# Layer 0's output product: seven half-size products for the prompt tiles, a plain one for the sample tile

## The chip, the core and the metric

The kernel runs on one core of one Trainium2 chip. A core has a matrix engine (TensorE, "PE" in the profile, with its weight loads as "PEld"), a vector engine (VectorE, "DVE"), a scalar engine (ScalarE, "ACT"), GpSimd ("POOL") and SyncE ("SP"), which issues the DMAs. Each works through its own queue in order; waits on semaphores tie the queues together. Operands lie in SBUF, 128 partitions wide; PE writes its results to PSUM, eight banks of 512 float columns, called `PB[0]` to `PB[7]`. The metric is the device time of one execution in microseconds (us).

## What is computed

One step of a two-layer encoder on 512 prompt rows and 128 sample rows (8 requests of 16). Layer 0 is a gated MLP, layer 1 an attention layer. After its mixer each layer multiplies by an output matrix, norms the result, adds it to the residual, and adds a gated embedding:

```python
def gmlp_branch(h, w_in, ln_g, ln_b, w_s, b_s, w_out):
    ...
    y = u * s.reshape(B, T, E) * jax.nn.silu(z)
    return y @ w_out, v
...
        xp = xp + rms_norm(op, norm_post[i])
        xs = xs + rms_norm(os_, norm_post[i])
        xp = xp + jax.nn.sigmoid(xp @ ple_w_gate[i]) * (p_prompt[i] @ ple_w_proj[i])
        xs = xs + jax.nn.sigmoid(xs @ ple_w_gate[i]) * (p_sample[i] @ ple_w_proj[i])
```

The change is about `y @ w_out` of layer 0: y has 640 rows (five tiles of 128: tiles 0 to 3 the prompt, tile 4 the sample) and 2048 columns, `w_out` is 2048 x 1024.

## The kernel before

All products are made from float32 values cut into a coarse part ("hi") and a rest ("lo"). `split` (L272 and L273) does it: ACT copies the source into a rounded type, DVE subtracts the copy from the source. `mm3` (L258 to L260) then issues three matmuls, hi by hi, hi by lo and lo by hi; each loads 128 columns of the left operand as weights of the array and streams up to 512 columns of the right one.

**Weights.** All weight blocks of the program stand in one list, `units`, in the order of use; a block is 256 rows by 512 columns (or 512 by 256) of float32, 512 KB. `fetch` issues its DMA (L119) into one of three raw buffers (`RAW`), `prefetch` splits it into one of five buffers in `W` (hi and lo, 1024 columns each), and `weights(n)` hands out the next n and asks for as many more as there are free buffers. So PE works on one buffer while up to four more are filled.

**Layer 0's mixer** is computed in pairs of 128-column groups, whose left factors are themselves made by seven half-size products: the sums of weight blocks are made by POOL (L200), the sums of results by DVE (L540 to L555). The last operations of a group are `gate_spatial` (L565 to L579), which leaves y in `R`, transposed: for each of 16 groups g of 128 columns of y a block of 128 partitions by 640 rows, `y0_at(g)`. The layout is that of the left operand, so a tile's 128 columns can be loaded as weights directly.

**The output product** is the first part of `tail(0, ...)`. For each half h of the 1024 output columns it runs over eight weight blocks (`kk`), in each over five row tiles t and two 128-row slices j of the block: 2 x 8 x 5 x 2 calls of `mm3`, accumulated in five PSUM banks. Before a block, `split_y` splits the y groups that it will need, each of 640 columns; each is split twice, once per half h. Ten transposes of the embedding input `p_prompt`, `p_sample` (L631) and five splits of it lie at the start of the product.

**Behind it** come, per tile: the squares and their sum (ACT, L704), the reciprocal root (DVE and POOL, L280 and L282), two scalings (DVE, L708, L709), two additions to the residual (L710, L711), eight transposes (L296) and their splits; then the product of the embedding (`embed`, 12 matmuls a tile), the gate product (48 matmuls a tile in two halves), and the norm in front of layer 1.

What decides the order on an engine is not the text alone: a scheduler places the instructions on each engine's queue along a modelled timeline, within what the data allow. `order` in the listings below is the result of that for one engine. Buffers come free in the order of use, so a late split holds up the DMA behind it, and a late matmul the split behind it.

Of the kernel before, what the change touches and what calls it, by code (L numbers as in the profile page):

```python
# [17 lines left out]
F32 = mybir.dt.float32  # L18
# [6 lines left out]
P = 128  # L25
D = 1024
# [31 lines left out]
def hybrid_trunk(tc, x_prompt, x_sample, ck, cv, clf, p_prompt, p_sample, norm_pre, norm_post,  # L58
# [19 lines left out]
    def second(name, dt):  # L78

        pool = tc.alloc_tile_pool(name=name, bufs=1, reuse_waits="tile")  # L80
        return pool, pool.tile([P, 10240], dt, name=name + "_t")
# [8 lines left out]
    def r1(o, n, p=P):  # L90
        return R1[:p, o:o + n]

    def f(ap):
        return ap.bitcast(F32)
# [3 lines left out]
    def ring(name, lst):  # L98
        i = counters.get(name, 0)
        counters[name] = i + 1  # L100
        return lst[i % len(lst)]

    def bank(lst=(0, 1, 2, 3, 4, 5, 6, 7)):
        return PB[ring(("bank", lst), lst)]

    def small(n=1, keep=False):

        name, first, end = ("kept", 0, 172) if keep else ("small", 172, N_SMALL)
        i = counters.get(name, first)
        if i + n > end:  # L110
            assert not keep
            i = first
        counters[name] = i + n
        return SML[:, i:i + n]
# [3 lines left out]
    def dma(out, in_):  # L118
        behind["sp"] = nc.sync.dma_start(out=out, in_=in_)  # L119
# [12 lines left out]
    def u_rows(w, r0, c0, k, n):  # L132
        units.append((w[r0:r0 + k * P, c0:c0 + n].rearrange("(k p) n -> p k n", p=P), k))
# [9 lines left out]
    def u_tail(wout, layer):  # L143
        for h in range(2):
            for kk in range(8):
                u_rows(wout[0], kk * 256, h * 512, 2, 512)
        for h in range(2):
            u_rows(w_proj[layer], 0, h * 512, 2, 512)
        for h in range(2):
            for kk in range(4):  # L150
                u_rows(w_gate[layer], kk * 256, h * 512, 2, 512)

    u_tail(g_wout, 0)
    joined = set()
    for p in range(8):
        for part in (2, 1, 0, 3):
# [8 lines left out]
    S0, S1 = 16, 48  # L165
    items = []
    for i in range(len(units)):
        if not S0 <= i < S1:
            items.append((i, None))
        elif i % 2 == 0:  # L170
            items += [(i, j) for j in range(4)]

    n0 = S1 + 16 + 2 + 8
    few = range(n0, n0 + 64 + 12)
    place, last_use = [], [-1] * (2 * NW)
    state = {"raw": 0, "used": 0}

    def raw_of(i):
        if S0 <= i < S1:
            z = (i - S0 + 1) % 4  # L180
            if z == NRAW:
                return r1(o_X, 1024)
        else:
            z = i % NRAW if i < S0 else (i + 1) % NRAW
        return RAW[:, z * 1024:z * 1024 + 1024]

    def fetch(upto):
        while state["raw"] < min(upto, len(units)):
            ap, k = units[state["raw"]]
            dma(raw_of(state["raw"]).rearrange("p (k n) -> p k n", k=k), ap)  # L190
            state["raw"] += 1

    def left_operands(i, j):
# [6 lines left out]
                nc.gpsimd.tensor_tensor(out=o, in0=a, in1=b, op=op)  # L200
        return (a11, SF[:, :1024], SF[:, 1024:2048], raw_of(i + 1))[j]

    def prefetch(upto, i0=0):

        while len(place) < min(upto, len(items)):
            i = len(place)
            u, j = items[i]
            taken = {z for k in range(i0, i) for z in place[k]}
            step = 1 if j == 0 else 2
            free = [z for z in range(0, 2 * (NW - (u in few)), step) if not taken & set(range(z, z + step))]  # L210
            if not free:
                return
            z = min(free, key=lambda z: max(last_use[z:z + step]))
            place.append(range(z, z + step))
            last_use[z:z + step] = [i] * step
            fetch(u + 1 if j is None else u + 2)
            o, n = z * 1024, step * 512
            hi, lo = W[:, o:o + n], W[:, o + n:o + 2 * n]
            if u in joined:
                k = units[u][1]  # L220
                hi, lo = (W[:, o:o + 2 * n].rearrange("p (k z n) -> p z k n", z=2, k=k)[:, z] for z in range(2))
                split(hi, lo, raw_of(u).rearrange("p (k n) -> p k n", k=k))
            elif j is None:
                split(hi, lo, raw_of(u))
            else:
                split(*((x.rearrange("p (k n) -> p k n", k=4) for x in (hi, lo)) if j == 0 else (hi, lo)), left_operands(u, j))
                if u > S0:
                    fetch(u + 4)

    def weights(n):  # L230

        i0 = state["used"]
        state["used"] += n
        prefetch(i0 + 2 * NW, i0)
        res = []
        for i in range(i0, i0 + n):
            u, j = items[i]
            k, o, m = units[u][1], place[i][0] * 1024, len(place[i]) * 512
            if u in joined:
                res.append(W[:, o:o + 2 * m].rearrange("p (k n) -> p k n", k=k))  # L240
                continue
            if j in (1, 2):
                views = [W[:, o + z:o + z + m].rearrange("p (a k n) -> p k a n", a=2, k=k) for z in (0, m)]
            else:
                views = [W[:, o + z:o + z + m].rearrange("p (k n) -> p k n", k=k) for z in (0, m)]
            res.append(tuple(views))
        return res
# [8 lines left out]
    def mm3(out, lhs, rhs, start, stop):  # L256
        (lh, ll), (rh, rl) = lhs, rhs
        nc.tensor.matmul(out, lh, rh, start=start, stop=False)  # L258
        nc.tensor.matmul(out, lh, rl, start=False, stop=False)  # L259
        nc.tensor.matmul(out, ll, rh, start=False, stop=stop)  # L260
# [9 lines left out]
    def split(hi, lo, src):  # L270

        nc.scalar.activation(out=hi, in_=src, func=AF.Copy)  # L272
        nc.vector.tensor_tensor(out=lo, in0=src, in1=f(hi), op=ALU.subtract)  # L273

    def rstd_of(ss, eps, mean=False, keep=False):
        t = small()
        if mean:
            nc.vector.tensor_scalar(out=t, in0=ss, scalar1=eps, scalar2=None, op0=ALU.add)
        else:
            nc.vector.tensor_scalar(out=t, in0=ss, scalar1=1.0 / D, scalar2=eps, op0=ALU.mult, op1=ALU.add)  # L280
        q = small(keep=keep)
        nc.gpsimd.tensor_tensor(out=q, in0=t, in1=mhalf, op=ALU.pow)  # L282
        return q

    def tok_rows(prompt, sample, t):
        return prompt[t * P:(t + 1) * P] if t < 4 else sample
# [42 lines left out]
    def run(steps):  # L329

        while True:
            try:
                next(steps)
            except StopIteration as e:
                return e.value
# [15 lines left out]
    def r2(o, n, p=P):  # L351
        return R2[:p, o:o + n]
# [173 lines left out]
    def y0_at(g):  # L526

        return r1(g // 4 * 2560, 2560).rearrange("p (t n) -> p t n", t=NT)[:, :, (g % 4) * P:(g % 4 + 1) * P]
# [207 lines left out]
                    xn = r1(o_xn + (t % 2) * D, D)  # L736
                    norm_to_hT(x1[t], xn, xn, gpre, t, (5, 6, 7))

    tail(0, lambda g, half: y0_at(g), (0, 1, 2, 3, 4))


    PRJ, ATT = (0, 1, 2, 3), (4, 5, 6)
# [428 lines left out]
```

## Time and profile before

| | us |
|---|---|
| median of 3 runs | 1315.37 (1315.31 to 1315.43) |
| the profiled execution: its own time | 1315.17 |
| the profiled execution: span from the first to the last instruction | 1313.4 |
| DVE busy in the span | 794.1 |
| ACT busy in the span | 553.1 |
| POOL busy in the span | 136.1 |

The mean granted clock of TensorE is 0.997 of the full one. The profile shows one execution: for each engine its busy time; windows of time with the busy time of each engine in them; groups of instructions of one line, operation and shape with their mean time; the timeline of single instructions; and the chain that ended last, which goes back from the end from each step to the one that released it. In a row `L273 DVE TENSOR_TENSOR W<-RAW,W 128x1024` stands for line 273, executed by DVE, writing the tile W from RAW and W, with 128 partitions and 1024 columns. `R` is the large buffer `R1`, `pb` a PSUM bank, `sf` and `r2x_t`, `r2b_t` are uses of a second buffer, `SML` holds scalars, one to a partition. A busy interval can overlap the next one of the same engine by a little.

### The profile page before, as it was taken

What the parts mean: (1) busy time and instruction counts of PE and PEld (TensorE: products, weight loads), DVE (VectorE), ACT (ScalarE), POOL (GpSimd) and SP (SyncE); (2) the same over time, 40 slices, a digit from 0 to 9 for tenths busy, and PEclk for the clock granted to TensorE, in tenths of its full rate; (3) what the DMA queues carried; (4) which work ended last, traced back from release to release, by engine and by line L of the source; (5) the groups of instructions that cost most, each with busy time, mean ns of one, the idle gap of its engine ahead of it and who ended that gap; (6) DMA issues with size and microseconds to landing.
All of it is one profiled execution on the core that took longest, in us unless ns stands there. A gap on an engine that the chain in (4) does not pass through costs nothing.

```text
span 1313.4 us, 20355 instructions
## 1 busy us (share of the span) xinstructions
PE 1304.7 (99%) x7683; PEld 1152.3 (88%) x7683; DVE 794.1 (60%) x1671; ACT 553.1 (42%) x1074; POOL 136.1 (10%) x144
## 2 busy tenths in 40 slices
PE   8999999999999999999999999999999999999998
PEld 6888999999988888888999889898988988888887
DVE  7744999999844455644555554556555566554543
ACT  5334555444535343533433334333434344435431
POOL 1012454543000000000000000000000000000100
PEclk8999999999999999999999999999999999999999
DMA  6432333232424213589676665788557687343211
GB/s 227 132 108 67 120 118 121 86 104 73 129 94 149 79 49 113 167 135 149 152 194 151 155 160 148 165 150 171 132 150 163 149 213 235 113 132 132 66 56 57
DMA packets 300053, 172.79 MB, mean 132 GB/s; under 512 B 188785, under 2 KB 269473, under 8 KB 299954
## 3 DMA queue, kind: packets, MB, share of 16 engines
q1 hardware_dynamic: 299810, 171.23, 49.3%
q8 instruction: 60, 0.98, 0.3%
q14 instruction: 39, 0.32, 0.1%
q10 hardware_dynamic: 144, 0.26, 0.1%
HBM read 149.86 MB, written 21.59 MB: 131 GB/s over the span
## 4 chain that ended last, share of the span: by engine, by line
PE 95%; DVE 3%; DMA 1%; issue 1%; ACT 0%; SPq 0%; POOL 0%; DVEq 0%
PE pb L258 22%; PE pb L260 22%; PE pb L259 22%; PE pb L324 7%; PE pb L867 6%; PE pb L325 3%; PE pb L868 3%; PE pb L986 3%; PE pb L979 1%; PE pb L1040 1%; PE pb L1066 1%; PE pb L296 1%; DVE W L273 1%; PE pb L571 1%; PE pb L1063 1%
## 5 line engine op out<-in xcount | busy, mean ns | idle before, releaser
L273 DVE TENSOR_TENSOR W<-RAW,W 128x1024 fp32r<-128x1024 f32 (+1 forms) x156 | 193.5, 1242 | 170.8 <-ACT W L272 136.5
L272 ACT ACTIVATE W<-RAW 128x1024 fp32r<-128x1024 f32 (+1 forms) x156 | 161.0, 1033 | 151.0 <-PE pb L260 47.5
L258 PE MATMUL pb<-A,W 128*128 128x384 f32 (+1 forms) x640 | 221.8, 347 | 0.0
L260 PE MATMUL pb<-A,W 128*128 128x384 f32 (+1 forms) x640 | 208.7, 326 | 0.0
L259 PE MATMUL pb<-A,W 128*128 128x384 f32 (+1 forms) x640 | 208.3, 325 | 0.0
L258 PE MATMUL pb<-W,A 128*128 128x512 f32 x520 | 205.0, 395 | 2.3 <-ACT A L272 2.3
L259 PE MATMUL pb<-W,A 128*128 128x512 f32 x520 | 203.7, 392 | 0.0
L260 PE MATMUL pb<-W,A 128*128 128x512 f32 x520 | 203.3, 393 | 0.1
L324 PE MATMUL pb<-A,W 128*128 128x512 f32 x384 | 150.7, 393 | 0.0
L258 PEld LDWEIGHTS pb<-A,W 128*128 128x128 f32 x640 | 120.4, 188 | 18.7 <-issue 8.9
L259 PEld LDWEIGHTS pb<-A,W 128*128 128x128 f32 x640 | 121.0, 189 | 0.7
L260 PEld LDWEIGHTS pb<-A,W 128*128 128x128 f32 x640 | 120.2, 188 | 0.1
L258 PEld LDWEIGHTS pb<-W,A 128*128 128x128 f32 x520 | 98.1, 189 | 22.3 <-ACT A L272 2.5
L867 PE MATMUL pb<-W,A 128*128 128x512 f32 x320 | 116.6, 403 | 0.0
L260 PEld LDWEIGHTS pb<-W,A 128*128 128x128 f32 x520 | 97.9, 188 | 20.9 <-DVE A L273 0.6
L259 PEld LDWEIGHTS pb<-W,A 128*128 128x128 f32 x520 | 98.0, 188 | 19.4
L325 PE MATMUL pb<-A,W 128*128 128x256 f32 x384 | 107.7, 280 | 0.0
L868 PE MATMUL pb<-W,A 128*128 128x256 f32 x320 | 89.5, 280 | 0.0
L273 DVE TENSOR_TENSOR A<-R,A 128x640 fp32r<-128x640 f32 (+1 forms) x51 | 41.0, 836 | 71.4 <-ACT A L272 70.7
L867 PEld LDWEIGHTS pb<-W,A 128*128 128x128 f32 x320 | 60.0, 188 | 15.1 <-DVE R L872 2.6
L325 PEld LDWEIGHTS pb<-A,W 128*128 128x128 f32 x384 | 72.1, 188 | 0.4 <-issue 0.4
L324 PEld LDWEIGHTS pb<-A,W 128*128 128x128 f32 x384 | 72.1, 188 | 0.2
(252 smaller groups left out, 2285.8 us busy)
## 6 DMA issues: line engine op xcount, KB each, us to landing
RAW<-in_fox_w_in SPq DMA_DIRECT2D x64, 512.0 KB
RAW<-in_gmlp_w_in SPq DMA_DIRECT2D x40, 512.0 KB
r2b_t<-in_cache_fox_v SPq DMA_DIRECT2D x32, 512.0 KB
r2b_t<-in_cache_fox_k SPq DMA_DIRECT2D x128, 128.0 KB
RAW<-in_gmlp_w_out SPq DMA_DIRECT2D x16, 512.0 KB
RAW<-in_ple_w_gate SPq DMA_DIRECT2D x16, 512.0 KB
RAW<-in_fox_w_out SPq DMA_DIRECT2D x16, 512.0 KB
out<-R SPq DMA_DIRECT2D x42, 128.0 KB
```

The costliest lines, as they stand in the source:

```text
L258: nc.tensor.matmul(out, lh, rh, start=start, stop=False)
L259: nc.tensor.matmul(out, lh, rl, start=False, stop=False)
L260: nc.tensor.matmul(out, ll, rh, start=False, stop=stop)
L272: nc.scalar.activation(out=hi, in_=src, func=AF.Copy)
L273: nc.vector.tensor_tensor(out=lo, in0=src, in1=f(hi), op=ALU.subtract)
L296: nc.tensor.transpose(out=b[:, j * P:(j + 1) * P], in_=src[:, (4 * c + j) * P:(4 * c + j + 1) * P], identity=ident)
L324: nc.tensor.matmul(out[1].rearrange("p (z n) -> p z n", z=2), w[0], h_both[:, :, k, SA:], start=k == 0, stop=False)
L325: nc.tensor.matmul(out[1][:, :TOK - SA], w[1], h_hi[:, k, SA:], start=False, stop=k == 7)
L571: nc.tensor.matmul(b0[:, t * P:(t + 1) * P], v_at(pnl, t)[:, c0:c0 + P], wm, start=True, stop=True)
L867: nc.tensor.matmul(b, hi, w, start=k == 0, stop=False)
L868: nc.tensor.matmul(b[:, :256], lo, w[:, :256], start=False, stop=k == 7)
L986: nc.tensor.matmul(O[:, d], v[:, j, hh * P:(hh + 1) * P], pt[:, j * P:(j + 1) * P], start=(j == 0), stop=(j == i))
```

## The change

The output product of layer 0 is made by a new function, `tail7`, in place of `tail(0, ...)`; layer 1 keeps `tail`. The four prompt tiles are taken as two halves (tiles 0 and 1, tiles 2 and 3), the 2048 columns of y as two halves, and the 1024 output columns as two halves. The product of these 2 x 2 by 2 x 2 blocks is made from seven half-size products instead of eight, with sums of blocks of y on the one side, sums of blocks of `w_out` on the other, and sums of results. A half-size product has 2 tiles x 8 slices, 16 calls of `mm3`. The sample tile is multiplied plainly, from the blocks that are there anyway.

The seven products come in three groups of 2, 3 and 2, each in four steps (`kk`). A step needs 3, 4 and 2 blocks of `w_out` (named by column half and row half, "21" is the second column half and the first row half), 36 blocks in all for 16 before. POOL makes the sums of weight blocks, in place, in the raw buffers (`out_operand`), which are eight now: three in `RAW` and five in a new use `r2o_t` of the second buffer; the first six blocks use `RAW` alone. DVE makes three of the four sums of y blocks (`sum1`, `sum3`, `sum2`), POOL the fourth (`sum4`, three operations). `parts_of` splits them into one of the slots in `A`. ACT and DVE bring results from PSUM to SBUF and add them up (`leave`). Tiles 2 and 3, complete after the second group, are normed during the last step but one of the third group.

```diff
+    def u_out7(wout):
+        for names in (("11", "21", "22"), ("11", "21", "22", "12"), ("12", "22")):
+            for kk in range(4):
+                out7[len(units)] = names
+                for n in names:
+                    u_rows(wout[0], ((int(n[1]) - 1) * 4 + kk) * 256, (int(n[0]) - 1) * 512, 2, 512)
...
     def raw_of(i):
-        if S0 <= i < S1:
+        if S2 <= i < S3:
+            z = (i - S2 + 1) % 3 if i < S2 + 6 else (i - S2 - 6 + 3) % 8
+            if z >= NRAW:
+                return r2((z - NRAW) * 1024, 1024)
+        elif S0 <= i < S1:
...
+    OUT_NEEDS = {"out30": 1, "out31": 3, "out40": 2, "out41": 3, "out42": 4, "out20": 1, "out21": 2}
+
+    def out_operand(u, j):
+        a = [raw_of(u + z) for z in range(len(out7[u]))]
+        sums = {"out31": (2, 1, 2, ALU.add), "out40": (1, 0, 1, ALU.subtract), "out41": (2, 2, 1, ALU.subtract),
+                "out42": (3, 3, 2, ALU.subtract)}
+        if j not in sums:
+            return a[int(j[-1])]
+        o, x, y, op = sums[j]
+        nc.gpsimd.tensor_tensor(out=a[o], in0=a[x], in1=a[y], op=op)
+        return a[o]
...
-            fetch(u + 1 if j is None else u + 2)
+            fetch(u + 1 if j is None else u + OUT_NEEDS.get(j, 2))
...
+            elif j in OUT_NEEDS:
+                split(hi, lo, out_operand(u, j))
...
-    tail(0, lambda g, half: y0_at(g), (0, 1, 2, 3, 4))
+    def tail7(layer, y_at):
...
+        def b_of(k, i, j):
+            return y_at(k + 8 * i)[:, 2 * j:2 * j + 2]
+        def sample_of(k, i):
+            return y_at(k + 8 * i)[:, 4:]
...
+        def sum1(k):
+            return parts_of(combine(nc.vector, scratch(), b_of(k, 0, 1), b_of(k, 0, 0)))
+        def sum3(k):
+            t3[k] = combine(nc.vector, scratch(), b_of(k, 1, 1), b_of(k, 0, 1))
+            return parts_of(t3[k])
+        def sum2(k):
+            return parts_of(combine(nc.vector, t3[k], t3[k], b_of(k, 0, 0), ALU.add))
+        def sum4(k):
+            o = combine(nc.gpsimd, scratch(), b_of(k, 1, 0), b_of(k, 1, 1))
+            combine(nc.gpsimd, o, o, b_of(k, 0, 1), ALU.add)
+            return parts_of(combine(nc.gpsimd, o, o, b_of(k, 0, 0)))
+        plain = lambda i, j: lambda k: parts_of(b_of(k, i, j))
+        stages = (
+            (((plain(0, 0), (0, 1)), (lambda k: parts_of(sample_of(k, 0)), (4,))), ((sum1, (2, 3)),)),
+            (((sum3, (0, 1)), (lambda k: parts_of(sample_of(k, 0), True), (4,))), ((sum2, (5, 6)),), ((plain(1, 1), (2, 3)),)),
+            (((lambda k: parts_of(sample_of(k, 1)), (7,)), (plain(1, 0), (5, 6))),
+             ((lambda k: parts_of(sample_of(k, 1)), (4,)), (sum4, (0, 1)))))
...
+        def leave(s, part):
+            for t in range(2):
+                if (s, part) == (0, 0):
+                    nc.scalar.activation(out=c_of(t, 0), in_=PB[t], func=AF.Copy)
+                elif (s, part) == (0, 1):
+                    nc.scalar.activation(out=c_of(t + 2, 1), in_=PB[2 + t], func=AF.Copy)
+                elif (s, part) == (1, 1):
+                    add(c_of(t + 2, 0), c_of(t, 0), PB[5 + t])
+                    add(c_of(t, 1), c_of(t + 2, 0), PB[t])
+                    add(c_of(t + 2, 0), c_of(t + 2, 0), c_of(t + 2, 1))
+                    add(c_of(t + 2, 1), c_of(t + 2, 1), c_of(t, 1))
+                elif (s, part) == (1, 2):
+                    add(c_of(t + 2, 0), c_of(t + 2, 0), PB[2 + t])
...
+        def out_steps():
...
+                            for _, banks in part:
+                                while len(left) < min(n + 9, len(todo)):
+                                    fn, k = todo[len(left)]
+                                    left.append(fn(k))
...
+                                for t, o in enumerate(banks):
+                                    ts = slice(t * P, (t + 1) * P)
+                                    mm3(PB[o], (hi[:, ts], lo[:, ts]), (w[0][:, j], w[1][:, j]), first, done)
...
+                    if (s, kk) == (2, 2):
+                        for t in (2, 3):
+                            normed(t)
...
+    tail7(0, y0_at)
```

The lines of the changed program stand elsewhere: `split` is L314 and L315, `mm3` L300 to L302, the sums of weight blocks L240, the sums of y blocks L844, the negative split of the sample L825 and L826, the sums of results L872, the gating L607 to L621 (L565 to L579 before). Three places in the queues follow.

DVE just ahead of the product; `L574` and `L616` are the same operation, the first gating of the last pair of groups. Before:

```order
L273 TENSOR_TENSOR W_63<-RAW_66,W_63 128x1024
L540 TENSOR_TENSOR R1_69<-R1_69,pb2_72 128x320
L273 TENSOR_TENSOR A_65<-R1_69,A_65 128x640 x2
L589 SCALAR_TENSOR_TENSOR R1_69<-sf_223,R1_69 128x320
L540 TENSOR_TENSOR R1_69<-R1_69,pb3_73 128x320
L574 SCALAR_TENSOR_TENSOR R1_69<-pb4_74,SML_68,sf_223 128x4x128
```

The same place in the changed program:

```order
L315 TENSOR_TENSOR W_63<-RAW_66,W_63 128x1024
L582 TENSOR_TENSOR R1_69<-R1_69,pb1_71 128x320
L631 SCALAR_TENSOR_TENSOR R1_69<-sf_223,R1_69 128x320
L315 TENSOR_TENSOR A_65<-R1_69,A_65 128x128
L315 TENSOR_TENSOR A_65<-R1_69,A_65 128x256 x2
L315 TENSOR_TENSOR A_65<-R1_69,A_65 128x128
L582 TENSOR_TENSOR R1_69<-R1_69,pb2_72 128x320
L631 SCALAR_TENSOR_TENSOR R1_69<-sf_223,R1_69 128x320
L582 TENSOR_TENSOR R1_69<-R1_69,pb3_73 128x320
L616 SCALAR_TENSOR_TENSOR R1_69<-pb4_74,SML_68,sf_223 128x4x128
```

The splits of whole y groups have become splits of two tiles (256 columns) and of the sample tile (128 columns).

DVE in the product, `W` the weight buffers and `A` the slots for parts of y. Before, early in it, with the embedding's splits (`pb5`, `pb6`, `pb7`) still among them:

```order
L273 TENSOR_TENSOR W_63<-RAW_66,W_63 128x1024
L273 TENSOR_TENSOR A_65<-pb6_76,A_65 128x2x128
L273 TENSOR_TENSOR A_65<-pb7_77,A_65 128x2x128
L273 TENSOR_TENSOR A_65<-R1_69,A_65 128x640 x2
L273 TENSOR_TENSOR W_63<-RAW_66,W_63 128x1024
```

In the changed program, where the splits for the second group begin:

```order
L315 TENSOR_TENSOR W_63<-r2o_t_2985,W_63 128x1024
L826 SCALAR_TENSOR_TENSOR A_65<-R1_69,A_65 128x128
L315 TENSOR_TENSOR A_65<-r2o_t_2985,A_65 128x256
L826 SCALAR_TENSOR_TENSOR A_65<-R1_69,A_65 128x128
L315 TENSOR_TENSOR W_63<-r2o_t_2985,W_63 128x1024
L844 TENSOR_TENSOR r2o_t_2985<-r2o_t_2985,R1_69 128x256
L315 TENSOR_TENSOR A_65<-r2o_t_2985,A_65 128x256 x2
L315 TENSOR_TENSOR A_65<-R1_69,A_65 128x256
L844 TENSOR_TENSOR r2o_t_2985<-r2o_t_2985,R1_69 128x256
L315 TENSOR_TENSOR W_63<-r2o_t_2985,W_63 128x1024
```

Between two weight splits stand about as many operations as before, of smaller shape, and PE has 12 or 18 matmuls to a weight split where it had 30.

POOL from the last sum of the mixer's weights on. Before, it next makes the reciprocal roots behind the product:

```order
L200 TENSOR_TENSOR sf_223<-R1_69 128x512
L200 TENSOR_TENSOR sf_223<-R1_69,RAW_66 128x512
L200 TENSOR_TENSOR sf_223<-sf_223,R1_69 128x512
L200 TENSOR_TENSOR sf_223<-RAW_66,sf_223 128x512
L282 TENSOR_TENSOR SML_68<-SML_68 128x1 x9
```

In the changed program stand behind the same four sums six sums of weight blocks, and then:

```order
L240 TENSOR_TENSOR r2o_t_2985<-r2o_t_2985 128x1024 x3
L240 TENSOR_TENSOR RAW_66<-RAW_66 128x1024
L240 TENSOR_TENSOR RAW_66<-RAW_66,r2o_t_2985 128x1024
L240 TENSOR_TENSOR r2o_t_2985<-r2o_t_2985,RAW_66 128x1024
L240 TENSOR_TENSOR r2o_t_2985<-r2o_t_2985 128x1024 x2
L844 TENSOR_TENSOR r2o_t_2985<-R1_69 128x256 x2
L240 TENSOR_TENSOR r2o_t_2985<-r2o_t_2985 128x1024
L844 TENSOR_TENSOR r2o_t_2985<-r2o_t_2985,R1_69 128x256
```

All 40 of POOL's new sums stand there, 16 of weight blocks and 24 of y blocks, where it had none in the product.

More of the change, by code (lines that the diff above doesn't have):

```diff
@@ L151, in u_tail, with u_embed @@
                 u_rows(w_gate[layer], kk * 256, h * 512, 2, 512)
-    u_tail(g_wout, 0)
+    out7 = {}
+    def u_out7(wout):
[4 more added lines that the diff above has]
+                    u_rows(wout[0], ((int(n[1]) - 1) * 4 + kk) * 256, (int(n[0]) - 1) * 512, 2, 512)
+    def u_embed(layer):
+        for h in range(2):
+            u_rows(w_proj[layer], 0, h * 512, 2, 512)
+        for h in range(2):
+            for kk in range(4):
+                u_rows(w_gate[layer], kk * 256, h * 512, 2, 512)
+    S2 = len(units)
+    u_out7(g_wout)
+    S3 = len(units)
+    u_embed(0)
+    S4 = len(units)
     joined = set()
@@ L167, in hybrid_trunk @@
     for i in range(len(units)):
-        if not S0 <= i < S1:
+        if S2 <= i < S3:
+            if i in out7:
+                items += [(i, "out%d%d" % (len(out7[i]), z)) for z in range(3 if len(out7[i]) == 4 else 2)]
+        elif not S0 <= i < S1:
             items.append((i, None))
@@ L171, in hybrid_trunk @@
             items += [(i, j) for j in range(4)]
-    n0 = S1 + 16 + 2 + 8
-    few = range(n0, n0 + 64 + 12)
+    few = range(S4, S4 + 64 + 12)
     place, last_use = [], [-1] * (2 * NW)
@@ L178, in raw_of @@
     def raw_of(i):
-        if S0 <= i < S1:
+        if S2 <= i < S3:
+            z = (i - S2 + 1) % 3 if i < S2 + 6 else (i - S2 - 6 + 3) % 8
+            if z >= NRAW:
+                return r2((z - NRAW) * 1024, 1024)
+        elif S0 <= i < S1:
             z = (i - S0 + 1) % 4
```

123 lines of the change are left out of this document (added).

## The prediction

> **What bounds the kernel now.** I read the page first, for which engine is full, then the windows of the stretch that the change touches, and last the chain that ended last inside it.
>
> ```profile
> span 1313.4 us, 20355 instructions
> PE 1304.7 (99%) x7683; PEld 1152.3 (88%) x7683; DVE 794.1 (60%) x1671; ACT 553.1 (42%) x1074; POOL 136.1 (10%) x144
> 346.30:456.70 110.40, 110.40 (x495) 91.39 (x494) 51.01 (x68) 42.97 (x69) 1.48 (x2) 1.00 0.34 113
> ```
>
> The first two rows are the page's: TensorE (PE) is busy in 99% of the span. The third is a row of the windows (length, then PE, weight loads, DVE, ACT and POOL busy, granted clock, DMA share, GB/s): in the 110.4 us of layer 0's output product PE never rests, DVE works 51 us, ACT 43, POOL 1.5. So today this stretch lasts as long as its matmuls. A busy PE is no measure of its speed; the chain gives the step:
>
> ```profile
> 346.54 0.23 PE pb L258
> 346.77 0.23 PE pb L259
> ...
> 351.10 0.23 PE pb L260
> 351.33 0.45 PE pb L258 x2
> ```
>
> From 346.54 to 351.33 lie 21 matmuls of 512 columns: 0.228 us each. The product has 2 halves x 8 weight blocks x 5 tiles x 2 x 3 = 480 of them, 109.4 us; with the ten transposes of the embedding input (1.1 us) it starts at 346.54 and ends near 457.1.
>
> **What the change removes.** Five tiles by sixteen row blocks by two column halves were 160 triples. Now seven products of two tiles by eight blocks are 112 and the sample 32: 144 triples, 432 matmuls. 48 x 0.228 = **10.9 us less of PE**. If PE stayed the bound, that would be the whole answer, so the question is whether the other engines keep up with 98.5 us of matmuls.
>
> **What it adds.** Steps of DVE come from these rows; a reported DVE time overlaps the next one by 0.08 (1.21 at 244.87, next start 246.00), so a step is the mean less 0.08.
>
> ```profile
> L273 DVE TENSOR_TENSOR W<-RAW,W 128x1024 fp32r<-128x1024 f32 x25 | 30.6, 1225 | 19.4 <-ACT W L272 18.4
> L920 DVE SCALAR_TENSOR_TENSOR R<-R,r2b_t 128x256 f32<-128x256 f32 x16 | 6.8, 425 | 4.5 <-ACT R L919 3.9
> L579 DVE TENSOR_TENSOR R<-R 128x640 f32<-128x640 f32 x16 | 13.8, 861 | 0.0
> L710 DVE TENSOR_TENSOR R<-R 128x512 f32<-128x512 f32 x10 | 6.9, 687 | 0.0
> L708 DVE SCALAR_TENSOR_TENSOR R<-pb,SML,R 128x512 f32<-128x512 f32 x10 | 7.5, 749 | 0.9 <-POOL SML L282 0.8
> L1033 POOL TENSOR_TENSOR R<-R,CST 128x16 f32<-128x16 f32 x16 | 4.3, 267 | 164.6 <-DMA R<-cs_sc 164.6
> L272 ACT ACTIVATE W<-RAW 128x1024 fp32r<-128x1024 f32 x16 | 16.8, 1048 | 11.6 <-PE pb L260 11.1 <-ACT R L704 0.5
> ```
>
> Weight operands: 16 splits become 28, 1.14 us of DVE each. Tile operands: instead of 32 splits of 640 columns there are 56 of 256 columns (0.34, as L920) and 32 of 128 (0.20, see 251.16 below), and 24 sums of 256 (0.34). POOL, idle here so far, gets 16 sums of 1024 columns and 24 of 256. No POOL sum of these widths has been run; between 16 columns (0.267, L1033) and 512 (1.30, next fence) a column costs 2.08 ns, which gives 2.36 and 0.77 us. From below they cannot cost less than the 1.30 and 0.27 of those smaller rows; from above, two sums of 512 are 2.60, one of 512 is 1.30. I take the line between the two rows. By engine all this still fits into 98.5 us: DVE some 85, POOL 56, ACT 28 x 1.05 and the small copies, near 65. DMA rises from 16 to 36 blocks of 512 KB.
>
> **But DVE and POOL don't work side by side.** The next rows are the timeline of a stretch in which both run (start, duration, engine, line), DVE first and POOL below.
>
> ```profile
> 244.87 1.21 DVE L273 TENSOR_TENSOR W<-sf,W 128x1024 fp32r<-128x1024 f32 x1
> 246.00 0.47 DVE L540 TENSOR_TENSOR R<-R,pb 128x320 f32<-128x320 f32 x1
> ...
> 247.97 1.96 DVE L273 TENSOR_TENSOR W<-RAW,W 128x1024 fp32r<-128x1024 f32 x1 [0.50 <-ACT W L272]
> 249.85 0.87 DVE L540 TENSOR_TENSOR R<-R,pb 128x320 f32<-128x320 f32 x2
> 250.64 0.59 DVE L512 SCALAR_TENSOR_TENSOR sf<-sf,SML,R 128x128 f32<-128x128 f32 x1
> 251.16 0.28 DVE L513 TENSOR_TENSOR R<-CST,R 128x128 f32<-128x128 f32 x1
> 251.36 0.34 DVE L512 SCALAR_TENSOR_TENSOR R<-R,SML 128x128 f32<-128x128 f32 x1
> ...
> 247.55 1.30 POOL L200 TENSOR_TENSOR sf<-sf,RAW 128x512 f32<-128x512 f32 x1
> 248.92 2.16 POOL L200 TENSOR_TENSOR sf<-RAW,sf 128x512 f32<-128x512 f32 x1
> ```
>
> The weight split issued at 247.97, in the middle of a POOL sum, takes 1.96 instead of 1.22 and ends 1.08 after that sum (248.85): it stood still until POOL was through. The next sum is issued at 248.92, during the split, and takes 2.16 instead of 1.30: it ends 1.23 after the split's step (249.85). L512 then takes 0.59 instead of 0.34, waiting for POOL again. The two L540, which read a PSUM bank, run at their usual pace beside POOL. So a DVE operation with two SBUF inputs and a POOL sum exclude each other and take turns; their times add. [...]
>
> Nearly all that the change adds to DVE has two SBUF inputs. By block pair, in us, beside PE:
> - first group: 2 x 1.14 + 6 x 0.34 + 2 x 0.20 = 4.7 of DVE, one sum of POOL 2.4: **7.1**; PE 30 x 0.228 = **6.8**
> - second: 3 x 1.14 + 10 x 0.34 + 2 x 0.20 = 7.2, and 3 x 2.36 = 7.1: **14.3**; PE 42 x 0.228 = **9.6**
> - third: 2 x 1.14 + 4 x 0.34 + 4 x 0.20 = 4.4, and 6 x 0.77 = 4.6: **9.0**; PE 36 x 0.228 = **8.2**
>
> In every group the shared work is longer than PE's, most in the second. Five weight buffers let it run ahead by about one pair, no more.
>
> **The sum.** It is made against the profiled execution, 1315.17 us around a span of 1313.4; the median of the runs shown, 1315.37, is 0.2 off, so both may be compared with the result. Now what stands ahead of the product on DVE:
>
> ```profile
> 332.73 2.35 DVE L273 TENSOR_TENSOR W<-RAW,W 128x1024 fp32r<-128x1024 f32 x2
> ...
> 344.19 1.56 DVE L273 TENSOR_TENSOR A<-R,A 128x640 fp32r<-128x640 f32 x2
> 345.66 0.49 DVE L589 SCALAR_TENSOR_TENSOR R<-sf,R 128x320 f32<-128x320 f32 x1
> 346.06 0.49 DVE L540 TENSOR_TENSOR R<-R,pb 128x320 f32<-128x320 f32 x1
> 346.46 0.75 DVE L574 SCALAR_TENSOR_TENSOR R<-pb,SML,sf 128x512 f32<-128x512 f32 x1
> ```
>
> Until 346.46 DVE has almost no gap. In the changed order three weight splits and twelve tile splits, six of 128 and six of 256 columns, stand ahead of that same L574 (four and six of 640 columns before, more time), and POOL's first two sums fall there too. I put L574 at 347.5. Behind it, until the last weight split of the product, two-input DVE work is 28 x 1.14 + 80 x 0.34 + 32 x 0.20 = 65.5, less those fifteen (3.4 + 1.2 + 2.0) = 58.9; the gating of the last pair, four steps of 0.78 (as L579) and two of 0.41 (as L589), 3.9; four sums of parts 2.4 (0.61 as L710); two steps of the early norm 1.3 (as L708 less 0.08; the rest of it comes behind): 66.5. POOL: 14 x 2.36 + 24 x 0.77 = 51.5. Together **118.0**, so the last split is done at 465.5, and PE has one part of 18 matmuls, 4.1, behind it: 469.6. Against 457.1 today that is **+12.5**, as a bare sum without a gap. Two things come on top. DVE work that reads PSUM (the embedding's five splits 1.7, six of the sums of parts 3.7, the rest of the gating 1.9: 7.3) hides only where POOL happens to hold the port; I take half, 3.6. And a split waits for ACT's copy (the 0.50 at 247.97 above): with 0.35 for each of 25 that is 8.8, again hidden where POOL has work; I take half, 4.4. 12.5 + 3.6 + 4.4 = **+20.5**: 1335.7. Both hidden gives 1327.7, none hidden 1343.8. Two POOL sums that hold up the seven half-products of layer 0 before the product would add up to 4.7 more, 1348.5.
>
> At nothing I cost the following. The tile norms: tiles 2 and 3 early, tiles 0, 1 and 4 behind the product, where PE has the embedding (60 matmuls, 13.7 us) and the gate of tiles 2 and 3 (48, 10.9) in front of them, against 3 us of DVE a tile; without that cover it would be some 9 us. The sums of parts: PSUM banks are read behind 12 to 18 other matmuls. The DMAs on SP's queue: 36 x 0.524 MB over 120 us is 157 GB/s, and eight raw buffers run ahead.
>
> **The rivals.**
> - *PE stays the bound*: POOL and DVE miss each other because the lookahead lets POOL sum while DVE idles. Then 1315.2 - 10.9 = **1304**. For it speaks the window of layer 0's half-products below, where PE is full beside 25.9 us of DVE and 13.5 of POOL in 28. Against it: there, as the rows above show, about every second operation of DVE reads PSUM and costs POOL nothing; here the sums by group exceed PE's in all three, so no order of them fits. It decides the other way from where POOL and two-input DVE work together fall under 98.5 us; I count 118. Chance 0.11.
>
> ```profile
> 234.00:262.00 28.00, 28.00 (x199) 27.98 (x198) 25.86 (x40) 12.69 (x24) 13.48 (x9) 1.00 0.30 93
> ```
>
> - [...] Chance 0.06.
> - *Worse than the sum*: DVE's queue, in order, stands behind a POOL sum whose ACT copy follows, with nothing hidden: **1346**. Chance 0.22.
> - *DMA bound in the second group*: 16 blocks of 0.524 MB in 38.2 us is 220 GB/s, where this stretch moved 113. It would cost less than the shared work, which stretches that group to 57 us, 147 GB/s; so it is hidden and has no chance of its own.
>
> **How the numbers follow.** Forecast 1336 (1328 to 1344 its own range) 0.61; the others as above. The range goes to 1349 on top, and down to 1316, which leaves out the faster case, most of the even one and a tail of the worst one, 0.18. A measurement here can tell 0.2% (2.6 us) from no change: faster 0.11, same 0.06, slower 0.83.
>
> **What would show it.** In the changed profile weight splits of DVE should show durations near 3.5 (1.2 and a POOL sum of 2.4), POOL's sums up to 3.5; PE should have gaps that end with a split of W or A, most of them in the second group, which should last near 57 us instead of 38; the first and third near 30 and 36. The product should end near 478 and the rest follow unchanged in length. I am wrong if splits keep 1.22 beside POOL, if PE has no gaps, or if the gaps end with DMA or with the norms.

## The result and the profile after

The changed kernel takes 1336.91 us (median of 6 runs, 1336.54 to 1338.2) beside 1315.45 of the kernel before on the same chip: ratio 1.0164, 95% interval 1.015 to 1.0178. It is 1.6% slower; the forecast was 1336. One execution of the kernel before (1431.27 us) and one of experiment 5 (1834.91) fell into a slower state and are left out of the ratios.

First the two rows of the page that answer to those of before:

```profile
span 1334.8 us, 20594 instructions
PE 1305.6 (98%) x7635; PEld 1148.4 (86%) x7635; DVE 866.6 (65%) x1779; ACT 569.4 (43%) x1142; POOL 218.5 (16%) x184
```

The span grew by 21.4 us, and TensorE is busy for 0.9 us more, although 48 matmuls are gone. The windows of the product say where (length, then PE, weight loads, DVE, ACT and POOL busy, granted clock, DMA share, GB/s). The first row is the whole product, less its last 1.3 us. The next three are the groups, cut where PE begins the 41st and the 97th of the 144 triples of matmuls. The last row lies behind PE's last rest.

```profile
346.20:476.20 130.00, 107.86 (x437) 84.91 (x437) 122.30 (x170) 59.59 (x127) 77.27 (x40) 0.92 0.52 170
345.90:382.70 36.80, 30.49 (x133) 24.77 (x132) 36.80 (x57) 17.30 (x38) 19.54 (x7) 0.91 0.71 243
382.70:435.70 53.00, 43.19 (x169) 33.06 (x168) 49.62 (x56) 27.02 (x58) 48.00 (x27) 0.94 0.51 162
435.70:477.50 41.80, 35.78 (x148) 28.42 (x147) 37.48 (x63) 15.58 (x31) 9.73 (x8) 0.92 0.35 112
447.00:477.00 30.00, 30.00 (x129) 24.71 (x128) 25.68 (x47) 12.97 (x25) 3.54 (x2) 0.96 0.27 88
```

Before, PE was busy through all of its 110.4 us here. Now it rests 22.1 of 130: 6.3 in the first group, 9.8 in the second, 6.0 at the start of the third. In these stretches DVE is nearly full and POOL, idle before, is at work. The waits of PE name who ended each rest (waiting line, releaser, us in total, times, longest):

```profile
PE pb L301 <- DVE W L315: 9.1, 6, 2.6
PE pb L809 <- DVE A L315: 6.3, 1, 6.3
PE pb L300 <- DVE R L872: 2.5, 1, 2.5
PE pb L302 <- DVE A L315: 1.8, 1, 1.8
PE pb L300 <- ACT A L314: 1.2, 1, 1.2
PE pb L300 <- ACT R L893: 1.2, 1, 1.2
```

19.7 of the 22.1 us end with DVE: a weight split, an operand's split, the embedding's split (L809 are its transposes) or a sum of parts. None ends with a DMA or a norm. The timeline shows why DVE is late (start, duration, engine, line; the first five rows DVE, then POOL):

```profile
365.00 5.38 DVE L844 TENSOR_TENSOR r2o_t<-R 128x256 f32<-128x256 f32 x3
370.30 0.74 DVE L315 TENSOR_TENSOR A<-pb,A 128x256 fp32r<-128x256 f32 x2
...
387.39 3.39 DVE L315 TENSOR_TENSOR W<-r2o_t,W 128x1024 fp32r<-128x1024 f32 x1
...
394.25 1.21 DVE L315 TENSOR_TENSOR W<-r2o_t,W 128x1024 fp32r<-128x1024 f32 x1
...
407.35 2.45 DVE L315 TENSOR_TENSOR W<-r2o_t,W 128x1024 fp32r<-128x1024 f32 x1 [3.38 <-ACT W L314]
...
364.89 2.39 POOL L240 TENSOR_TENSOR r2o_t<-r2o_t,RAW 128x1024 f32<-128x1024 f32 x1
...
387.14 2.55 POOL L240 TENSOR_TENSOR RAW<-RAW,r2o_t 128x1024 f32<-128x1024 f32 x1
394.62 11.61 POOL L240 TENSOR_TENSOR r2o_t<-r2o_t,RAW 128x1024 f32<-128x1024 f32 x1 [4.92 <-DMA r2o_t<-in_gmlp_w_out]
...
416.18 0.77 POOL L844 TENSOR_TENSOR r2o_t<-r2o_t,R 128x256 f32<-128x256 f32 x1
```

The split at 387.39 takes 3.39, the one at 394.25, which starts with no POOL sum under way, 1.21: the first stood still for POOL's sum of 387.14 (to 389.69) and ended 1.09 after it. Three y sums (365.00) fill 5.38 us instead of 1.1 beside POOL's weight sums; the embedding's split stands behind them in DVE's queue (370.30), and PE's longest rest, 6.31 us to 370.76, is the wait for it. The long row of POOL, 11.61 at 394.62, is a sum that stood still in its turn: it ends at 406.23, after DVE has run out of work, and DVE rests 3.38 for ACT's copy of it. POOL's own prices are the estimated ones: 2.39 and 0.77.

Not foreseen was what a rest costs afterwards. The chain behind two of the rests, and the granted clock around the four stretches where it falls (windows, columns as above):

```profile
433.15 0.50 PE pb L301
433.65 0.24 PE pb L302
...
445.03 0.79 PE pb L300
445.83 0.43 PE pb L301
446.25 0.43 PE pb L302
...
449.24 0.36 PE pb L300
449.60 0.23 PE pb L301
```

```profile
370.00:376.00 6.00, 5.24 (x18) 4.31 (x19) 6.00 (x14) 5.71 (x13) 0.00 (x0) 0.64 0.28 89
394.00:400.00 6.00, 6.00 (x21) 4.75 (x20) 6.00 (x14) 3.21 (x6) 5.38 (x1) 0.72 0.84 266
418.00:424.00 6.00, 4.47 (x12) 3.23 (x12) 6.00 (x5) 4.56 (x11) 6.00 (x5) 0.72 0.57 168
445.00:451.00 6.00, 5.97 (x17) 4.77 (x18) 6.00 (x12) 1.49 (x3) 0.00 (x0) 0.63 0.17 67
```

Behind four of the eleven rests a matmul takes 0.43 instead of 0.23 for 3 to 4 us. Busy time times what the clock lacks is 1.9 + 1.7 + 1.3 + 2.2 = 7.0 us. And the first matmul behind a rest takes some 0.3 longer than the next ones (0.50 at 433.15, 0.79 at 445.03), an estimated 3 us for eleven rests. The result is then 22.1 of rests and some 10 of slower matmuls against the 10.9 saved, which makes the 21.4. (Experiment 1 below, with the same matmuls and no rest, has PE busy for 1295.2 us, 10.4 less.) Behind the product nothing changed: the gate's last matmul ends 21.6 us later than before, the program 21.4.

### The profile page after: what moved, and what is told of

It is laid out like the page before. It is cut to its first block, busy times and chain, and to the rows that moved or that the text cites. A ratio compares the mean times of both kernels' runs of the same rounds, so it can differ in the third digit from the quotient of the medians.

```text
span 1334.8 us, 20594 instructions
## 1 busy us (share of the span) xinstructions
PE 1305.6 (98%) x7635; PEld 1148.4 (86%) x7635; DVE 866.6 (65%) x1779; ACT 569.4 (43%) x1142; POOL 218.5 (16%) x184
## 4 chain that ended last, share of the span: by engine, by line
PE 89%; DVE 5%; issue 3%; POOL 1%; ACT 1%; DMA 0%; DVEq 0%; POOLq 0%; ACTq 0%
PE pb L300 20%; PE pb L301 19%; PE pb L302 19%; PE pb L366 7%; PE pb L1107 6%; PE pb L367 3%; PE pb L1108 3%; PE pb L1226 3%; DVE W L315 2%; PE pb L338 1%; PE pb L1219 1%; PE pb L1280 1%; PE pb L1306 1%; DVE r2o_t L844 1%; DVE A L315 1%
## 5 line engine op out<-in xcount | busy, mean ns | idle before, releaser
L315 DVE TENSOR_TENSOR W<-RAW,W 128x1024 fp32r<-128x1024 f32 (+1 forms) x152 | 190.0, 1252 | 157.1 <-ACT W L314 120.6
L300 PE MATMUL pb<-A,W 128*128 128x384 f32 (+1 forms) x640 | 221.7, 346 | 0.0
L314 ACT ACTIVATE W<-RAW 128x1024 fp32r<-128x1024 f32 (+1 forms) x152 | 156.9, 1033 | 149.2 <-PE pb L302 44.2
L301 PE MATMUL pb<-W,A 128*128 128x512 f32 x504 | 200.8, 399 | 9.1 <-DVE W L315 9.1
L302 PE MATMUL pb<-A,W 128*128 128x384 f32 (+1 forms) x640 | 208.6, 326 | 0.0
L300 PE MATMUL pb<-W,A 128*128 128x512 f32 x504 | 200.9, 402 | 5.6 <-DVE R L872 2.5
L302 PE MATMUL pb<-W,A 128*128 128x512 f32 x504 | 198.9, 398 | 1.8 <-DVE A L315 1.8
L300 PEld LDWEIGHTS pb<-A,W 128*128 128x128 f32 x640 | 120.4, 188 | 18.5 <-issue 8.9
L301 PEld LDWEIGHTS pb<-W,A 128*128 128x128 f32 x504 | 96.5, 192 | 30.7 <-DVE W L315 11.7
L302 PEld LDWEIGHTS pb<-A,W 128*128 128x128 f32 x640 | 120.2, 188 | 0.2
L300 PEld LDWEIGHTS pb<-W,A 128*128 128x128 f32 x504 | 96.8, 192 | 27.2 <-DVE R L872 2.9
L1107 PE MATMUL pb<-W,A 128*128 128x512 f32 x320 | 116.3, 402 | 0.0
L302 PEld LDWEIGHTS pb<-W,A 128*128 128x128 f32 x504 | 96.6, 192 | 22.4 <-DVE A L315 2.2
L1259 POOL COPY r2b_t<-R 128x64 f32<-128x64 f32 x32 | 11.9, 372 | 381.4 <-PE pb L1280 316.8
L1107 PEld LDWEIGHTS pb<-W,A 128*128 128x128 f32 x320 | 60.0, 188 | 15.0 <-DVE R L1112 3.1
```

The lines of the kernel that those rows point to most:

```text
L1107: nc.tensor.matmul(b, hi, w, start=k == 0, stop=False)
```

## The experiments

The theory: DVE operations with two SBUF inputs and POOL sums exclude each other, so their times add. ("Port" in the prediction and the expectations is a name for this; what the two engines share inside the chip no run shows.) Rivals: PE waits for the chain of steps (a split waits for its sum, whoever makes it), for the DMAs, or for DVE's own added work. "Before" is 1315.06 us in the first four experiments, 1315.24 in the next four, 1315.07 in the next three and 1315.32 in the last.

**1. No sum on POOL.** Weight sums and the fourth y sum are left out (splits take the raw blocks); all DMAs, splits and DVE sums stay.

```diff
-        nc.gpsimd.tensor_tensor(out=a[o], in0=a[x], in1=a[y], op=op)
...
-            return parts_of(combine(nc.gpsimd, o, o, b_of(k, 0, 0)))
+            return parts_of(b_of(k, 1, 0))
```

> Leaves out all 40 of POOL's sums in the product: the weight blocks and the y block are split as they lie. Blocks, DMAs, splits, matmuls and the rest stay. Shared port (the forecast's reason): 66.5 us of two-input work of DVE and 7.3 of other DVE work are left for 98.5 us of matmuls, so PE is the bound: 1304 to 1307. DMA too late (36 blocks where there were 16; POOL's waits in the changed profile often end with a DMA): nothing changes, over 1330. DVE's own load (122 of 130 us busy): the same sums of DVE remain, so over 1325.

Measured: 1304.32 us. Its window of the product:

```profile
346.20:444.60 98.40, 98.40 (x440) 81.37 (x439) 83.61 (x167) 60.23 (x125) 3.54 (x2) 1.00 0.62 215
```

PE never rests, beside 83.6 us of DVE and the 36 blocks' DMAs at 215 GB/s. The whole loss comes with POOL's forty sums; the DMAs and DVE's own added work cost nothing.

**2. Weight sums made, but used by nobody.** From the seventh block on the sums go to an unused place and the splits take the raw blocks, so the product lacks these sums: POOL's load without the chain. The y sums on POOL stay as they are.

```diff
-        nc.gpsimd.tensor_tensor(out=a[o], in0=a[x], in1=a[y], op=op)
+        nc.gpsimd.tensor_tensor(out=a[o] if u < S2 + 6 else r2(8704, 1024), in0=a[x], in1=a[y], op=op)
```

> POOL makes the same 40 sums, but from the seventh block on the weight sums go to an unused place and the splits take the blocks as they lie: POOL's load stays, and the way from a block through POOL to its split is gone for 14 of 16. Shared port: the load decides, so 1330 to 1338. Rival, the added step on the way of a block (DMA, POOL, ACT, DVE one behind the other): with the step gone 1305 to 1315.

Measured: 1336.42 us, as the changed kernel. Waits of PE:

```profile
PE pb L301 <- DVE W L315: 19.3, 5, 6.9
PE pb L300 <- DVE R L872: 4.3, 1, 4.3
```

No weight split of the later blocks waits for a sum any more, and PE rests as long, 23.6 us: load, not chain.

**3. The chain without the reading.** Each weight sum becomes two POOL memsets of the block, so the products are of constants. The step and its waits stay (1.9 us for 2.4), but POOL reads nothing; the y sums on POOL stay.

```diff
-        nc.gpsimd.tensor_tensor(out=a[o], in0=a[x], in1=a[y], op=op)
+        for _ in range(2):
+            nc.gpsimd.memset(a[o], 0.5)
```

> Each weight sum is two memsets of POOL on the same block (0.96 us each by the profile before), so the step through POOL stays, with 1.9 us for 2.4, but it reads nothing; the products are then of constants. Shared port, if only reading POOL operations take it: 14 x 2.36 less of shared work, 118 - 33 = 85, so PE is the bound, 1305 to 1310. Step on the way: little is gained, 1330 or more.

Measured: 1306.53 us, with a single rest of 1.8 us. So a POOL step of the same place and waits that reads nothing is nearly free here: 2.2 us over experiment 1, with the y sums on POOL in it.

**4. All sums on DVE**, the fourth as one operation, from the second, which is kept.

```diff
-        nc.gpsimd.tensor_tensor(out=a[o], in0=a[x], in1=a[y], op=op)
+        nc.vector.tensor_tensor(out=a[o], in0=a[x], in1=a[y], op=op)
...
-            t3[k] = combine(nc.vector, scratch(), b_of(k, 1, 1), b_of(k, 0, 1))
+            t3[k] = combine(nc.vector, r2(6656 + k * 256, 256).rearrange("p (t n) -> p t n", t=2), b_of(k, 1, 1), b_of(k, 0, 1))
...
-            o = combine(nc.gpsimd, scratch(), b_of(k, 1, 0), b_of(k, 1, 1))
-            combine(nc.gpsimd, o, o, b_of(k, 0, 1), ALU.add)
-            return parts_of(combine(nc.gpsimd, o, o, b_of(k, 0, 0)))
+            return parts_of(combine(nc.vector, scratch(), b_of(k, 1, 0), t3[k]))
```

> Computes the whole. The weight sums go to DVE (1.14 us each where POOL needs 2.36), and the fourth y sum becomes one subtraction on DVE, as block (1,0) less the kept sum2, instead of three on POOL. Shared port: 66.5 + 14 x 1.14 + 8 x 0.34 = 85 us, with the PSUM work 92.5, under 98.5: 1304 to 1309, faster than both kernels. DVE's own load as the cause: 19 us more on it, so slower than the changed kernel, 1340 or more.

Measured: 1310.47 us (6 runs), ratio 0.9965 (0.9953 to 0.9978), faster than both kernels, though 1.5 above the expected range. Its windows, by group (a few matmuls of one group stand among those of the next):

```profile
346.20:376.20 30.00, 28.62 (x130) 22.74 (x129) 30.00 (x62) 17.79 (x41) 0.00 (x0) 1.00 0.84 284
376.20:417.50 41.30, 39.42 (x171) 31.30 (x170) 41.30 (x77) 25.98 (x52) 0.00 (x0) 1.00 0.66 214
417.50:451.20 33.70, 33.68 (x150) 27.53 (x149) 31.72 (x56) 16.52 (x32) 1.10 (x2) 1.00 0.42 133
```

DVE is now full itself in the first two groups, and PE rests 3.3 us there; the clock stays at 1.00.

**5 to 7. How much, and which.** The weight sums alone on DVE (5: the first change of experiment 4), the fourth y sum alone (6: the other two), and all on DVE with the fourth in three operations as it was (7).

> The sixteen weight sums move from POOL to DVE, the fourth y sum stays on POOL with three operations; the result is the reference's. Shared port, times add: the shared work behind L574 was 118.0; 14 x 2.36 = 33 of POOL leave it and 14 x 1.14 = 16 of DVE come, so 101 beside 98.5 of PE, most of what is left on DVE, where nothing has to take turns with a 1024-column sum: 1306 to 1316, I say 1311. Rival, the y sums on POOL are what holds the splits up (24 operations, each a turn): it stays above 1328. Rival, DVE is the bound by its own load as soon as it has the weight sums: as in the fourth kernel, 1310 or a little more.

> The weight sums stay on POOL; the fourth y sum becomes one DVE operation (block minus the kept second sum) for three of POOL; the result is the reference's. Shared port, times add: 24 x 0.77 = 18.5 leave the shared work and 8 x 0.34 = 2.7 come: 102.2 instead of 118.0, so some 16 less than the changed kernel's 1336.9: 1321, range 1314 to 1327. Rival, each group by itself: the y sums belong to the third group, which was not late, so nothing is won: 1334 to 1338. Rival, the weight sums alone are the cause, 1024 columns at a time: the same 1335.

> All forty sums on DVE, the fourth y sum still three operations; the result is the reference's. Against the kernel with all sums on DVE and one operation for the fourth (1310.5) DVE has 16 x 0.34 = 5.4 more, all in the third group, where it had no PE gap to show. Shared port (only the sum of DVE and POOL counts): DVE 66.5 + 16 + 8.2 = 91 of two-input work and 7 of PSUM work against 98.5 of PE: 1310 to 1316, I say 1312. Rival, the step counts and not the engine (forty sums must cost whoever makes them): above 1325.

Measured: 1322.71, 1324.92 and 1312.67 us. 7 is as expected; 6 is in its range but 4 us above what I said, and 5 is 12 above and outside its range. (Of those 12, 8 are the PSUM work and copies that the prediction puts on top and my sum for 5 left out.) Each kind of sum on POOL costs about the same: over experiment 4, the y sums 12.2 (5), the weight sums 14.5 (6), and both 26.4 (the changed kernel) against 26.7 added up. In 5 POOL's rows show something that the theory lacks (first POOL, then DVE):

```profile
389.39 17.62 POOL L844 TENSOR_TENSOR r2o_t<-R 128x256 f32<-128x256 f32 x1 [72.07 <-PE pb L301]
407.09 0.73 POOL L844 TENSOR_TENSOR r2o_t<-r2o_t,R 128x256 f32<-128x256 f32 x1
...
389.46 0.43 DVE L315 TENSOR_TENSOR A<-R,A 128x256 fp32r<-128x256 f32 x1
...
405.99 0.42 DVE L844 TENSOR_TENSOR r2o_t<-r2o_t,R 128x256 f32<-128x256 f32 x1
409.68 0.48 DVE L315 TENSOR_TENSOR A<-r2o_t,A 128x256 fp32r<-128x256 f32 x1 [3.27 <-ACT A L314]
```

A sum of 0.73 us stood for 17.62, until DVE's unbroken row of two-input operations ended at 406.4. Is this shutting out the loss?

**8. The norms back behind the product**, in the kernel of experiment 4.

```diff
-                    if (s, kk) == (2, 2):
-                        for t in (2, 3):
-                            normed(t)
...
-            if t not in (2, 3):
-                normed(t)
+            normed(t)
```

> The kernel with all sums on DVE (1310.5), with tiles 2 and 3 normed behind the product, as the other three, instead of during its last group; the result is the reference's. The prediction costs the early norm at nothing and says that the norms behind the product are covered by the embedding and the gate: 1309 to 1312. Rival, the early norm is what keeps the start of the gate from waiting: two tiles of 3 us each come onto the path, 1313 to 1317. Rival, the early norm itself takes DVE from the splits of the third group: 1307 to 1309.

Measured: 1310.47 us, the same. Early or late, two norms cost nothing here.

**9 to 11. Breaks in DVE's row.** Sixteen tiny DVE memsets, which read nothing, in the kernels of 5 (9), of the change (10) and of 4 (11, the control):

```diff
         def sum3(k):
+            nc.vector.memset(r2(8704, 8), 0.0)
...
         def sum2(k):
+            nc.vector.memset(r2(8704, 8), 0.0)
```

> The fifth kernel (weight sums on DVE, y sums on POOL, 1322.7) with one DVE memset of 128x8 put before each of the sixteen second and third y sums, so among its two-input operations; nothing reads it, the result is the reference's. In the fifth kernel POOL's first y sum of 0.73 took 17.62 and went on when DVE came to stand. Theory, a stream of two-input DVE operations without a break keeps the port, and any operation that does not need it lets POOL in: no POOL sum of 256 columns over 5 us, the PE gap of 4.4 us gone or short, 1313 to 1318. Rival, only a real rest of DVE or a PSUM operand lets POOL in: a POOL sum of over 12 us and a time of 1322 to 1325. Rival, POOL was not shut out but waited for its operands: as the second.

> The changed kernel (1336.9) with the same sixteen memsets of DVE; the result is the reference's. Shared port, times add: letting POOL in earlier takes the sum of 11.61 us down to 5 or less, but the shared work stays 118, so most of the loss stays: 1331 to 1338, I say 1335. Rival, the shutting out of POOL is most of the loss and the adding up little: below 1325.

> The kernel with all sums on DVE (1310.5) with the same sixteen memsets: their own price, with no POOL sum to let in. Sixteen operations of 128x8 with a step of about 0.07 us: 1 us where DVE is full, so 1310 to 1312; the result is the reference's.

Measured: 1322.99, 1337.0 and 1310.85 us: none differs from its kernel without breaks. Yet in 9 the y sum of 17.62 is gone; the same place (POOL, then DVE):

```profile
389.70 1.65 POOL L844 TENSOR_TENSOR r2o_t<-R 128x256 f32<-128x256 f32 x2 [72.28 <-PE pb L301]
...
386.85 1.21 DVE L315 TENSOR_TENSOR W<-r2o_t,W 128x1024 fp32r<-128x1024 f32 x1
386.87 0.07 DVE L851 MEMSET r2o_t<- 128x8 f32 x1
...
389.79 0.96 DVE L844 TENSOR_TENSOR r2o_t<-r2o_t,R 128x256 f32<-128x256 f32 x1
```

and in 10 POOL's sum of 11.61 took 3.12:

```profile
395.50 3.12 POOL L240 TENSOR_TENSOR r2o_t<-r2o_t,RAW 128x1024 f32<-128x1024 f32 x1 [4.94 <-DMA r2o_t<-in_gmlp_w_out]
```

POOL is let in, but in 9 the DVE operations that it gets in front of now take 0.96 instead of 0.41. My theory for 9 (a gain of 5 to 10 us) fell: what POOL no longer waits, DVE does. Whose turn it is does not matter in these two kernels, the sum does. That the memsets let POOL in is not shown as strictly: at 389.70 none stands beside it, and the scheduler's order around it changed a little too.

**12. A forecast by the sum.** From the prediction's terms the shared work S of each kernel can be worked out: 66.5 of DVE (1), 85 with the y sums on POOL (3), 85.2 (4), 90.7 (7), 101 (5), 102.2 (6), 118 (changed, 2). With all 16.1 us of PSUM work and ACT waits on top, of which the prediction took half, the time would be 1304.3 + S + 16.1 - 98.5, or 1304.3 where that is less: 1304.3, 1306.9, 1307.1, 1312.6, 1322.9, 1324.1 and 1339.9. Measured: 1304.3, 1306.5, 1310.5, 1312.7, 1322.7, 1324.9 and 1336.9. This was worked out after those runs, so one more was to test it: experiment 4 with eight of the weight sums on POOL.

```diff
-        nc.vector.tensor_tensor(out=a[o], in0=a[x], in1=a[y], op=op)
+        eng = nc.gpsimd if j in ("out40", "out41") else nc.vector
+        eng.tensor_tensor(out=a[o], in0=a[x], in1=a[y], op=op)
```

> The kernel with all sums on DVE (1310.5), but with two of the three weight sums of each step of the second group back on POOL, eight of sixteen; the result is the reference's. The runs so far follow one sum: time = 1304.3 + what two-input DVE work and POOL's sums take together over 98.5 us of matmuls, with all 16.1 us of PSUM work and copies on top, where the prediction took half. Here 66.5 + 2.7 for the fourth y sum + 6 x 1.14 + 8 x 2.36 = 94.9, and 94.9 + 16.1 - 98.5 = 12.5: 1316.8, range 1314 to 1320. Rival, half on top as predicted (8.0): 4.4, so 1308.7, under 1312. Rival, splits and sums of one step that cross between two engines cost more than their lengths: above 1322.

Measured: 1321.11 us, 4.3 above the rule and just outside its range; half on top (1308.7) is far off. Its longest wait of PE:

```profile
PE pb L301 <- ACT W L315: 4.7, 1, 4.7
```

The rule takes the product as one pool, but these sums all fall into the second group. By that group alone, in the prediction's manner, a step has 7.2 + 1.14 of DVE and 2 x 2.36 of POOL, 13.1 for 9.6 of PE: four steps are 13.9 us late even with nothing on top, 1318.2. That is nearer, but the trace does not bear it out. PE's rests are 8.5 us in all, and its busy time is 8.5 longer than in experiment 1, much of that at a lower clock (windows of two stretches behind rests):

```profile
376.00:385.00 9.00, 7.45 (x17) 5.11 (x18) 9.00 (x7) 6.15 (x16) 7.30 (x3) 0.62 0.46 140
400.00:409.00 9.00, 6.25 (x16) 4.94 (x17) 9.00 (x9) 5.93 (x12) 4.96 (x2) 0.62 0.34 108
```

And here the shutting out comes before rests of its own. Two POOL sums stand until DVE, which needs them, has run out of other work (first POOL, then DVE):

```profile
365.57 9.16 POOL L241 TENSOR_TENSOR r2o_t<-r2o_t,RAW 128x1024 f32<-128x1024 f32 x1 [13.94 <-DMA r2o_t<-in_gmlp_w_out]
390.76 8.78 POOL L241 TENSOR_TENSOR r2o_t<-r2o_t,RAW 128x1024 f32<-128x1024 f32 x1 [5.24 <-DVE r2o_t L845]
...
374.76 1.23 DVE L241 TENSOR_TENSOR r2o_t<-r2o_t 128x1024 f32<-128x1024 f32 x1 [2.29 <-POOL r2o_t L241]
399.58 3.35 DVE L241 TENSOR_TENSOR r2o_t<-r2o_t 128x1024 f32<-128x1024 f32 x1 [2.26 <-POOL r2o_t L241]
```

Which part of the 4.3 is the group's own excess, which the shutting out and which the clock stays open: this kernel was not run with breaks. The sum is good to some 4 us.

## Why the prediction was right

*The removed matmuls.* 10.9 us were forecast for PE left alone, 1304: experiment 1 gives 1304.32.

*DVE and POOL exclude each other.* This carried the forecast, and 1 to 3 show it from three sides: without the sums no loss (1304.32 us), with unused sums all of it (1336.42 beside 1336.91), with a POOL step that doesn't read almost none (1306.53). Of the signs named, the gaps that end with W and A and the end of the product (477.5 for 478) are there. The others came in part. Of the 25 weight splits behind L616 one took 3.39, one 2.45, six about 1.75 and the rest 1.21; much of DVE's standing still fell on its shorter operations, as the 5.38 at 365.00. The second group has most of the gaps' time, but less than half, 9.8 of 22.1 us; the groups took 36.8, 53.0 and 41.8 us for 30, 57 and 36. And POOL's sums, named up to 3.5, reached 11.61.

*Durations.* POOL 2.39 and 0.77 (forecast 2.36 and 0.77), free splits 1.21 as before. The two are also the shortest of the changed kernel, so nothing here gives ground for an even result (0.06).

*The sum came out right partly because three errors cancel.* The last weight split of the product is this row of DVE:

```profile
460.73 1.21 DVE L315 TENSOR_TENSOR W<-RAW,W 128x1024 fp32r<-128x1024 f32 x1
```

- "Together 118.0, so the last split is done at 465.5": it is done at 461.9, 3.6 earlier; 1.1 of these because L574 (L616 now) came at 346.40, not 347.5.
- "Two things come on top", PSUM work and copies, 8.0: nothing of it shows at that place, since the 115.5 from 346.40 to 461.9 already hold them. (In the kernels with less POOL work most of the 16.1 does come on top.)
- "PE has one part of 18 matmuls, 4.1, behind it": PE ended at 477.5, 15.6 behind it, nearly four parts. -3.6 - 8.0 + 11.5 is 0. PE was that far behind because the rows of the groups took each group's POOL work as done in its own time, which it is not. POOL ran ahead and made most of the third group's y sums during the second (48.00 us of POOL in the second, 9.73 in the third). So behind 445.03 PE never rests (the row from 447.00), the splits are again ahead of it, further than the "about one pair" of the prediction, and PE, not the shared work, set the end.

*The first group* was to take 30 us and took 36.8: the 6.3 of the embedding's split, which reads PSUM and is not held up itself (the one of 379.79 takes its usual 0.41 beside a POOL sum from 379.73 on) but stands in line behind y sums that are, and the slow matmuls behind that rest. The prediction priced that split by its own 1.7 us, not by what is queued ahead of it.

*Not in the prediction at all:* the 7 us at half the rate and the some 3 of matmuls behind rests. The rests were forecast at 31.4 (20.5 + 10.9) and were 22.1, so 9 us of rests too many stand against 10 of slower matmuls that were not forecast. That the kernel would be slower, and by which mechanism, was foreseen; that 1336 was met within 1 us is luck.

*At nothing:* the DMAs (1) and the norms (8, in the kernel of 4) cost nothing, as said. The best kernel measured is that of experiment 4, 0.35% faster than before; 1304 was reached only without the sums.

## What to carry to other kernels

An idle engine is not a free one: before giving it work, look at what it can hold up on the busy one. Here POOL's forty sums cost 32.6 us (1336.91 beside 1304.32), because they and DVE operations with two SBUF inputs took turns and their times had to be added. Ask for each group of steps alone, too, whether that sum fits under the bound: the sum over the whole product was 4.3 us too low when the shared work lay in one group, though why is not shown. An operation that POOL does not hold up still waits for those that stand ahead of it in its queue, here the embedding's split, for which PE rested 6.31 us. And a rest of TensorE can cost more than its length, here 22.1 us of rests and some 10 behind them.

## What the runs showed of the hardware

- *A POOL sum can be shut out for long.* Sums of 2.4 and 0.73 us took 11.61 (changed kernel, 394.62) and 17.62 (experiment 5, 389.39) while DVE ran two-input operations back to back. Elsewhere the two alternate one by one, as in the changed kernel from 379.73 to 390.78, four sums of some 2.5 us beside four DVE operations of 2.28 to 3.39. The order of issue alone does not tell whose turn it is: the operations from 389.46 on in experiment 5 were issued after POOL's sum of 389.39 and went first. What decides between the two ways stays open; in experiments 9 and 10 these long waits were gone, at no gain (1322.99 and 1337.0 us).
- *The clock after short rests.* In the changed kernel half rate follows a rest of 6.31 us, but also rests that were each 2.6 us or less. Two of these stretches come behind several rests close together, the third (from 418.95) behind a single one of 2.56 us with 22.0 us of unbroken matmuls ahead of it (394.00 to 416.00). In the four windows above the granted clock is 0.64, 0.72, 0.72 and 0.63. In the product of experiment 4, with 3.3 us of rests in all and none above 1.4, it stayed at 1.00; what length of rest brings the slowdown these runs do not show.
